# Head 1's keys and queries projected plainly, input sums spread over more steps, splits dealt by chunk, one copy moved to ScalarE

## The chip, the core and the metric

One core of a Trainium2 chip runs the whole program. Its engines are the matrix engine (PE, with its weight loads shown as PEld), VectorE (DVE), ScalarE (ACT), GpSimd (POOL) and SyncE (SP), which issues the transfers between memory and the on-chip buffers. PE writes only to PSUM banks; DVE and ACT read them out. Each engine runs its own instructions in order and waits on semaphores for the others. The metric is device time in microseconds, the median of the timed runs; less is better.

## The reference

An encoder of two layers on 1024 tokens of width 1024, in float32. Layer 0 mixes tokens by neighbourhood attention, layer 1 by differential attention; each layer then has a gated convolutional channel mixer and a gated embedding. The change lies in layer 1's attention:

```python
def diff_attention(h, w_qkv, lam, subln_g, w_o, t5_table, lambda_init):
    q, k, v = jnp.split(h @ w_qkv, 3, axis=-1)      # 8 heads; q, k: two maps of 64, v: 128
    ...
        s = jnp.einsum('bhmqd,bhmkd->bhmqk', qb, k).astype(jnp.float32) + bias[None, :, None]
        a = jax.nn.softmax(s, axis=-1)
        w = a[:, :, 0] - lam_full * a[:, :, 1]
        return jnp.einsum('bhqk,bhkd->bhqd', w.astype(v.dtype), v)
    ...
    o = rms_norm(o, subln_g) * (1.0 - lambda_init)
    return o @ w_o
```

## The kernel before

**Precision.** A float32 product is computed as three matmuls of a reduced-precision type (`mm3`, L258 to L263): each operand is split into a high part (ACT, `high`, L224) and a low remainder (DVE, `low`, L227), and high x high, high x low and low x high are accumulated in one PSUM bank. Splits thus cost ACT and DVE one instruction each.

**Two programs interleaved on PE.** PE's order is written out by hand; the other engines' order is found by the compiler, by priority (the order in the program) and by its own estimate of when an operand is ready. `da` runs the attention in 64 *chunks* n (8 heads of 8 blocks of 128 queries): the scores of chunk n+1 (`da_scores`, L882), its softmax (DVE L704, ACT exponential L708, the difference of the two maps on DVE L895), the transposes of chunk n's weights in two groups of four (`da_turn`, L907; the first group copied out of PSUM by ACT, L910, the second by DVE, L912), the product with the values (`da_values`, L921, with ACT's squares L924, a DVE scalar L925, a POOL root L273 and a DVE scaling L927), and a transpose of the result (`da_out`, L935). Into it PE is given *steps* of the projections: `tick(part)` adds `part * self.rate` to a credit and takes one step of the generator `da_stream` for each whole unit of it. The rate is 6.5 steps a chunk for the first 16 chunks and 5.14 behind. A step is one `mm3` (L261, L262, L263), 512 tokens wide. `need` takes steps at once until a head's keys and queries (`self.qk`) or values (`self.v`) exist.

**The stream before.** `plain` projects one weight block by one half of the tokens in 8 steps. Head 0's keys and queries are plain (32 steps), then the values of heads 0 and 1 (32 steps). The rest is done in *pairs* (`PAIRS`): a pair of weight blocks is multiplied in 7 half-size products of 4 steps instead of 8 (a Strassen-like scheme), 28 steps for what takes 32. A pair's products need sums of weight quarters (`Pair.sums`, four POOL operations, L118 to L121), splits of seven stationary operands (`Pair.operand`), and sums of the outputs (`put`, L158 to L175). They also need twelve sums of input quarters, T1 to T4, made once, in `sums(n)`: POOL operations (L560 to L570) into `room`, splits into a ring of four slots, a store to memory (`stash`, L554), from where each pair loads them again (L616). `sums(0)` to `sums(8)` were called at fixed steps of the plain part: steps 18, 26, 30, 36, 42, 46, 52, 57 and 61, counted from the stream's start. Each call first emits the splits and stores of the sums of the call before.

**Jobs.** `self.jobs` is a list of small pieces of work (a split, say). `job(act, dve)` takes the first one and orders its ACT part behind the instruction `act` and its DVE part behind `dve`. Before, it is filled near the layer's end only (rows of the output weights, the embedding's operands) and called in two places a chunk: behind the difference of the maps (in `da_scores`) and behind the second copy (in `da_turn`). `hurry` takes a job at once.

**Turns.** Values come out of the projection transposed; a *turn* (L292, and a copy on ACT, L590) brings them to rows. Turns wait a given number of steps and then for the end of a chunk or for `need`.

Of the kernel before, what the change touches and what calls it, by code (L numbers as in the profile page):

```python
# [92 lines left out]
PAIRS = [("kq", 1), ("kq", 2), ("v", 2), ("kq", 3), ("kq", 4), ("v", 4), ("kq", 5), ("kq", 6), ("v", 6), ("kq", 7)]  # L93
# [5 lines left out]
class Pair:  # L99


    def __init__(self, trunk, W, room, kind, j):
        self.trunk, self.room, self.kind, self.j = trunk, room, kind, j
        self.src = (W[KT + j], W[j]) if kind == "kq" else (W[2 * KT + j], W[2 * KT + j + 1])
        self.A, self.o, self.ps = {}, {}, {}
        self.products = [PRODUCTS[n] for n in range(7)]

# [15 lines left out]
    def operand(self, q):  # L123
        k = self.products[q][0]
        self.o[k] = self.trunk.operand(self.A[k])
# [14 lines left out]
    def out(self, row, half, src, turns, turn, wait):  # L140

        k, j = self.trunk, self.j
        if self.kind == "v":
            turns.append([wait, turn(self.h[row], half, src, 2 * (j + row) + half)])
            return
        s = slice(half * 512, half * 512 + 512)
        if row:
            k.split(src, self.h[:, 0, s], self.h[:, 1, s], -0.125)
        else:
            k.split(src, self.h[:, 2, s], self.h[:, 3, s])  # L150

    def put(self, a, turns, turn):
# [12 lines left out]
        elif a == "S3":  # L165
            tt(out=w, in0=ps[1], in1=p1, op=ALU.add)
        elif a == "S1":
            act(c5, ps[2], AF.Copy)
            nc.gpsimd.tensor_tensor(out=w, in0=w, in1=c5, op=ALU.add)
            self.out(1, 1, w, turns, turn, 4)  # L170
        elif a == "A22":
            tt(out=p1, in0=ps[1], in1=p1, op=ALU.add)
            self.out(1, 0, p1, turns, turn, 3)
        else:
            tt(out=u, in0=ps[2], in1=u, op=ALU.add)  # L175
            self.out(0, 1, u, turns, turn, 3)
            if self.kind == "kq":
                self.trunk.qk[self.j] = self.h


class Trunk:
# [329 lines left out]
    def da_stream(self, hT, x, first, mid):  # L511
# [4 lines left out]
        turns = []  # L516

# [8 lines left out]
        def plain(w, tb, wait=None):  # L526
            s = slice(tb * 512, tb * 512 + 512)
            ps = self.bank(self.pj)
            for kt, _ in enumerate(self.proj(w, hT, ps, tb)):
                if wait:  # L530
                    wait(kt)
                step()
# [40 lines left out]
        def at(*steps):  # L573
            steps = dict(steps)
            return lambda kt: sums(steps[kt]) if kt in steps else None

        s, ps = yield from plain(wk, 0)
        self.split(ps, A[:, 2, s], A[:, 3, s])
        s, ps = yield from plain(wq, 0, mid)
        self.split(ps, A[:, 0, s], A[:, 1, s], -0.125)  # L580
        s, ps = yield from plain(wk, 1, at((2, 0)))
        self.split(ps, A[:, 2, s], A[:, 3, s])
        wv = self.wblock(W[2 * KT])
        s, ps = yield from plain(wq, 1, at((2, 1), (6, 2)))
        self.split(ps, A[:, 0, s], A[:, 1, s], -0.125)
        self.qk[0] = A

        def turn(v, g, src, way):
            def of():
                self.transposed(src, lambda _, t: nc.scalar.activation(v[:, 4 * g : 4 * g + 4], t, AF.Copy), groups=(0,))  # L590
                self.v[way] = v
            return of

        steps = [at((4, 3)), at((2, 4), (6, 5)), at((4, 6)), at((1, 7), (5, 8))]
        for j in range(2):
            v = self.page(x, "v", (P, KT, P), bufs=3)
            vT = self.page(self.raw, "raw")
            for tb in (0, 1) if j == 0 else (1, 0):
                s, ps = yield from plain(wv, tb, steps.pop(0))
                nc.scalar.activation(vT[:, s], ps, AF.Copy)  # L600
                turns.append([5, turn(v, tb, vT[:, s], 2 * j + tb)])
                if j == tb == 1:
                    for k in range(4):
                        self.split(room[:, k], B12[0][:, k], B12[1][:, k])
                    pairs = [Pair(self, W, room, *a) for a in PAIRS]
                    pairs[0].load(0), pairs[0].load(1)
                    pairs[0].sums()
            if j == 0:
                wv = self.wblock(W[2 * KT + 1])

        moving = {"B11": B11, "B21": B21, "T1": B12, "B22": B22}
# [8 lines left out]
        for k in range(4):  # L620
            load(k)
        for n in range(3):
            pairs[0].operand(n)
        for i, p in enumerate(pairs):
            last = i == len(pairs) - 1
            after = None if last else pairs[i + 1]
            p.begin(x)
            for q, (a, b, bank) in enumerate(p.products):
                if after and q == 5:
                    after.sums()  # L630
                if q + 3 < 7:
                    p.operand(q + 3)
                elif after:
                    after.operand(q - 4)
                if after and q in (1, 2):
                    after.load(q - 1)
                if last and q == 0:
                    emb = self.embeddings(1, x)
                if last and q in (0, 6):
                    next(emb)  # L640
                ps, first = p.bank(bank, q)
                for k in range(4):
                    mov = (ring[:, k, 0], ring[:, k, 1]) if b in stash else tuple(o[:, k] for o in moving[b])
                    o = p.o[a]
                    self.mm3(ps, (o[:, 0, k], o[:, 1, k]), mov, first and k == 0, k == 3, not first)
                    if b in stash:
                        load(k)
                    step()
                    yield
                p.put(a, turns, turn)  # L650

        yield
# [7 lines left out]
    def begin(self, stream):  # L660
        self.stream, self.qk, self.v, self.credit, self.rate, self.open = stream, {}, {}, 0.0, 6, False
        self.jobs = []
# [204 lines left out]
    def da_scores(self, x, n):  # L867
# [27 lines left out]
        done = nc.vector.scalar_tensor_tensor(out=w, in0=e[1], scalar=c, in1=w, op0=ALU.mult, op1=ALU.add).ins  # L895
        self.job(self.exp, done)

    def da_turn(self, x, n, g):
# [10 lines left out]
        if g == 0:  # L909
            self.turned_w = nc.scalar.activation(wT[:, 0:4], t, AF.Copy).ins  # L910
        else:
            self.job(self.turned_w, nc.vector.tensor_copy(wT[:, 4:8], t).ins)  # L912

    def da_values(self, x, n):
# [31 lines left out]
    def da(self, hT, oT, first, mid):  # L946
# [4 lines left out]
        with self.tc.tile_pool(name="xa1", bufs=2, reuse_waits="tile") as x:  # L951
# [5 lines left out]
            for n in range(N + 1):  # L957
                self.rate = 6.5 if n < 2 * NT else 5.14
# [95 lines left out]
    def hurry(self):  # L1054

        todo = self.jobs.pop(0)
        if todo:
            todo()

# [989 lines left out]
```

## Time and profile before

| what | us |
|---|---|
| timed runs: median (lowest, highest) | 2711.51 (2711.2, 2711.7) |
| the profiled execution, its time | 2708.44 |
| the profiled execution, its span | 2706.7 |
| layer 1's attention, first chunk's scores to last chunk's | 1308.8 to 1877.4 |

The span runs from the first to the last instruction of the program on the core; the execution's own time adds 1.7 us around it. All times below are microseconds from the span's start. A matmul's listed duration is its latency; matmuls overlap, so the distance from one start to the next is what it costs PE. A wait is listed with what released it.

### The profile page before, as it was taken

How to read it: one execution, taken by the hardware profiler on the slowest of the kernel's cores; microseconds unless marked ns; L12 is line 12 of the kernel's file. 1: busy time of each engine (PE TensorE's matmuls, PEld its weight loads, DVE VectorE, ACT ScalarE, POOL GpSimd, SP SyncE). 2: the span in 40 equal slices, each digit the busy share in tenths (PEclk: the TensorE clock that was granted, in tenths of full speed). 3: DMA queues.
4: the chain of work that ended last, by engine and by line, in shares of the span. 5: the costliest groups of instructions: out<-in, count | busy, mean ns of one | idle time of the engine just before them, and what ended most of it. 6: DMA issues, size and time to landing. Idle time of an engine off the chain costs nothing.

```text
span 2706.7 us, 37008 instructions
## 1 busy us (share of the span) xinstructions
PE 2660.8 (98%) x13372; PEld 2196.0 (81%) x13372; DVE 2021.1 (75%) x3442; ACT 1353.2 (50%) x2548; POOL 561.2 (21%) x531
## 2 busy tenths in 40 slices
PE   8999999999999999999899999999999999999999
PEld 6888887878888888888678787777878888888887
DVE  6777776699777767676788888886699777768674
ACT  5555556454444444454455556565454444444452
POOL 2221220003334300001732222100103333300000
PEclk9999999999999999999899999999999999999999
DMA  6223226423332373333365555552423333374342
GB/s 184 85 66 105 76 94 195 132 71 128 106 113 98 116 272 122 117 131 115 124 240 200 197 175 194 178 171 91 160 70 131 103 108 103 103 261 138 117 137 100
DMA packets 151515, 367.21 MB, mean 136 GB/s; under 512 B 14202, under 2 KB 41082, under 8 KB 151331
## 3 DMA queue, kind: packets, MB, share of 16 engines
q1 hardware_dynamic: 151330, 364.85, 41.0%
q8 instruction: 105, 1.72, 0.3%
q14 instruction: 80, 0.65, 0.1%
HBM read 284.08 MB, written 92.90 MB: 139 GB/s over the span
## 4 chain that ended last, share of the span: by engine, by line
PE 38%; DVE 6%; ACT 2%; issue 2%; DMA 1%; POOL 1%; SPq 0%; ACTq 0%; DVEq 0%; POOLq 0%
PE b L261 9%; PE b L262 8%; PE b L263 8%; PE g L1078 3%; PE m L1078 3%; PE b L921 2%; PE s L882 2%; DVE E L704 1%; PE b L907 1%; DVE E L895 1%; ACT E L708 1%; PE b L1078 1%; PE b L292 1%; DVE ws L227 1%; DVE r L227 0%
## 5 line engine op out<-in xcount | busy, mean ns | idle before, releaser
L261 PE MATMUL b<-r,ws 128*128 128x512 f32 (+1 forms) x1304 | 532.3, 408 | 1.7 <-DVE r L396 1.6
L262 PE MATMUL b<-r,ws 128*128 128x512 f32 (+1 forms) x1304 | 505.2, 387 | 0.6 <-DVE r L227 0.5
L263 PE MATMUL b<-r,ws 128*128 128x512 f32 (+1 forms) x1304 | 505.6, 388 | 0.0
L263 PEld LDWEIGHTS b<-r,ws 128*128 128x128 f32 x1304 | 246.1, 189 | 51.3
L261 PEld LDWEIGHTS b<-r,ws 128*128 128x128 f32 x1304 | 247.4, 190 | 47.5 <-issue 3.5
L708 ACT ACTIVATE E<-E,mn 128x1024 f32<-128x1024 f32 (+2 forms) x256 | 221.7, 866 | 121.2 <-DVE mn L704 120.0
L262 PEld LDWEIGHTS b<-r,ws 128*128 128x128 f32 x1304 | 247.9, 190 | 35.5 <-DVE r L227 1.9
L261 PE MATMUL b<-r,wa 128*128 128x512 f32 x688 | 268.2, 390 | 2.0 <-DVE B L1470 2.0
L263 PE MATMUL b<-r,wa 128*128 128x512 f32 x688 | 268.1, 390 | 0.0
L262 PE MATMUL b<-r,wa 128*128 128x512 f32 x688 | 267.9, 389 | 0.0
L261 PE MATMUL b<-r,r 128*128 128x512 f32 x648 | 254.5, 393 | 0.9 <-ACT ws L1835 0.6
L262 PE MATMUL b<-r,r 128*128 128x512 f32 x648 | 252.7, 390 | 0.0
L263 PE MATMUL b<-r,r 128*128 128x512 f32 x648 | 252.5, 390 | 0.0
L273 POOL TENSOR_TENSOR ss<-ss,mhalf 128x1 f32<-128x1 f32 x128 | 74.3, 581 | 790.8 <-DVE ss L269 383.1
L224 ACT ACTIVATE r<-raw 128x512 fp32r<-128x512 f32 (+1 forms) x168 | 108.6, 655 | 192.0 <-PE b L262 168.9
L227 DVE TENSOR_TENSOR ws<-raw,ws 128x512 fp32r<-128x512 f32 (+3 forms) x178 | 168.2, 951 | 46.4 <-ACT ws L224 44.2
L227 DVE TENSOR_TENSOR r<-raw,r 128x512 fp32r<-128x512 f32 (+1 forms) x168 | 124.4, 747 | 71.0 <-ACT r L224 67.7
L224 ACT ACTIVATE ws<-raw 128x512 fp32r<-128x512 f32 (+3 forms) x178 | 122.1, 692 | 109.0 <-PE b L263 53.3
L1078 PE MATMUL m<-r,ws 128*128 128x512 f32 x672 | 157.0, 392 | 0.0
L1078 PE MATMUL g<-r,ws 128*128 128x512 f32 x672 | 155.8, 391 | 0.0
L261 PEld LDWEIGHTS b<-r,wa 128*128 128x128 f32 x688 | 129.2, 188 | 29.9 <-DVE B L1470 3.2
L704 DVE CUSTOM_DVE_ANT_0 E<-s,T 128x1024 f32<-128x1024 f32 x128 | 151.1, 1217 | 1.7 <-PE s L882 1.7
(226 smaller groups left out, 5384.0 us busy)
## 6 DMA issues: line engine op xcount, KB each, us to landing
r<-stashT SPq DMA_DIRECT2D x120, 512.0 KB, 4.3
raw<-in_w_in SPq DMA_DIRECT2D x86, 512.0 KB, 3.5
raw<-in_qkv SPq DMA_DIRECT2D x48, 512.0 KB, 5.1
spillS<-r SPq DMA_DIRECT2D x88, 256.0 KB, 3.0
r<-in_ffn_w_out SPq DMA_DIRECT2D x40, 512.0 KB, 5.9
raw<-spillS SPq DMA_DIRECT2D x40, 512.0 KB, 3.6
spillA<-B SPq DMA_DIRECT2D x66, 256.0 KB, 2.9
raw<-spillA SPq DMA_DIRECT2D x30, 512.0 KB, 3.9
```

The lines of the kernel that those rows point to most:

```text
L224: return self.nc.scalar.activation(hi, src, AF.Copy).ins
L227: return self.nc.vector.tensor_tensor(out=lo, in0=src, in1=hi.bitcast(F32), op=ALU.subtract).ins
L261: mm(out, sta[0], mov[0], start=first, stop=False, skip_group_check=onto)
L262: mm(out, sta[0], mov[1], start=False, stop=False, skip_group_check=onto)
L263: mm(out, sta[1], mov[0], start=False, stop=last, skip_group_check=onto)
L273: self.nc.gpsimd.tensor_tensor(out=ss, in0=ss, in1=self.mhalf, op=ALU.pow)
L292: self.nc.tensor.transpose(t[:, k * P : k * P + P], h[:, c : c + P], self.ident)
L704: nc.vector.tensor_tensor_reduce(out=e, in0=s, in1=bias, scale=1.0, scalar=3e38, op0=ALU.add, op1=ALU.min, accum_out=mn)
L708: self.exp = nc.scalar.activation(e, e, AF.Exp, bias=mn, scale=-1.0, accum_out=sm).ins
L882: nc.tensor.matmul(s[m][:, w], A[o, a, q], A[o, b, w], start=z == 0, stop=z == 2)
L921: nc.tensor.matmul(o, wT[:, k], V[:, k], start=k == 0, stop=k == KT - 1)
L1078: mm(out[half], a, b[:, w], start=first and k + z == 0, stop=last and k == n - 1 and z == 2)
```

## The change

- The pair `("kq", 1)` goes; head 1's keys and queries are projected by `plain`, between the values of head 0 and those of head 1 (whose halves are done in the order 1, 0). The plain part is now 96 steps long instead of 64, and nine pairs follow instead of ten.
- `sums(0)` to `sums(8)` are called at steps 18, 26, 35, 44, 53, 61, 69, 76 and 84. The splits and stores of the sums of the call before become jobs; what is left of them is emitted at the next call (`all_jobs`).
- The first pair's weights are loaded at steps 66 and 78, its first operand and the splits of one input quarter become jobs at step 88, its sums of weights are made at step 91. Every later operand is a job as well, asked for three products ahead as before; an operand that is not there when its product begins is made at once.
- While the stream is in its plain and pair part (`self.third`), `da_values` deals a job too, behind the squares, so there are three places a chunk; and the second copy of turned weights is done by ACT instead of DVE.
- The second load of a pair's weights is issued two products later, and the sum `w` is added by whichever of its two parts comes last.
- The rates are 6.3 and 5.3 instead of 6.5 and 5.14.

```diff
-PAIRS = [("kq", 1), ("kq", 2), ("v", 2), ("kq", 3), ("kq", 4), ("v", 4), ("kq", 5), ("kq", 6), ("v", 6), ("kq", 7)]
+PAIRS = [("kq", 2), ("v", 2), ("kq", 3), ("kq", 4), ("v", 4), ("kq", 5), ("kq", 6), ("v", 6), ("kq", 7)]
...
     def operand(self, q):
-        k = self.products[q][0]
-        self.o[k] = self.trunk.operand(self.A[k])
+        k, trunk = PRODUCTS[q][0], self.trunk
+
+        def do():
+            self.o[k] = trunk.operand(self.A[k])
+            return trunk.did
+
+        trunk.jobs.append(do)
...
+        def put(m, key, t):
+            did = self.split(t, ring[:, m % 4, 0], ring[:, m % 4, 1])
+            nc.sync.dma_start(stash[key][m // 3], raw[:, m % 4])
+            return did
+
         def sums(n):

             k = n // 2
+            self.all_jobs()
             if made:
-                for m, key, t in made.pop():
-                    self.split(t, ring[:, m % 4, 0], ring[:, m % 4, 1])
-                    nc.sync.dma_start(stash[key][m // 3], raw[:, m % 4])
+                self.jobs += [lambda a=a: put(*a) for a in made.pop()]
...
+        plan = {u: lambda n=n: sums(n) for n, u in enumerate((10, 18, 27, 36, 45, 53, 61, 68, 76))}
+        plan |= {58: lambda: pairs[0].load(0), 70: lambda: pairs[0].load(1), 80: first_operands, 83: first_sums}
...
+        yield from keys(wk, A, 0)
+        yield from queries(wq, A, 0, mid)
+        yield from keys(wk, A, 1)
+        ws.append(self.wblock(W[2 * KT]))
+        yield from queries(wq, A, 1)
+        self.qk[0] = A
+        yield from values(ws.pop(), 0, (0, 1), W[KT + 1])
+        A = self.page(self.r2, "r2", (P, 4, SEQ), F32R)
+        wk = ws.pop()
+        yield from keys(wk, A, 0)
+        wq = self.wblock(W[1])
+        yield from keys(wk, A, 1)
+        yield from queries(wq, A, 0)
+        wv = self.wblock(W[2 * KT + 1])
+        yield from queries(wq, A, 1)
+        self.qk[1] = A
+        yield from values(wv, 1, (1, 0))
+        pairs[0].operand(2)
...
+            if after and q == 3:
+                self.all_jobs()
+                after.load(1)
+            if after and q == 5:
+                self.all_jobs()
+                after.sums()
+            if n + 3 < len(order):
+                order[n + 3][0].operand(order[n + 3][1])
...
+            while a not in p.o:
+                self.hurry()
...
         if g == 0:
             self.turned_w = nc.scalar.activation(wT[:, 0:4], t, AF.Copy).ins
+        elif self.third:
+            self.job(nc.scalar.activation(wT[:, 4:8], t, AF.Copy).ins, self.meant)
         else:
             self.job(self.turned_w, nc.vector.tensor_copy(wT[:, 4:8], t).ins)
...
-        nc.scalar.activation(os, o, AF.Square, scale=r0, accum_out=r)
-        nc.vector.tensor_scalar(out=r, in0=r, scalar1=1.0 / P, scalar2=EPS, op0=ALU.mult, op1=ALU.add)
+        squared = nc.scalar.activation(os, o, AF.Square, scale=r0, accum_out=r).ins
+        meant = nc.vector.tensor_scalar(out=r, in0=r, scalar1=1.0 / P, scalar2=EPS, op0=ALU.mult, op1=ALU.add).ins
         self.root(r)
+        if self.third:
+            self.job(squared, meant)
+        self.meant = meant
...
-                self.rate = 6.5 if n < 2 * NT else 5.14
+                self.rate = 6.3 if n < 2 * NT else 5.3
```

(The step numbers in `plan` are counted from the stream's ninth step.)

More of the change, by code (lines that the diff above doesn't have):

```diff
@@ L104, in __init__ @@
         self.src = (W[KT + j], W[j]) if kind == "kq" else (W[2 * KT + j], W[2 * KT + j + 1])
-        self.A, self.o, self.ps = {}, {}, {}
-        self.products = [PRODUCTS[n] for n in range(7)]
+        self.A, self.o, self.ps, self.made, self.w = {}, {}, {}, [], 0
     def load(self, n):
@@ L571, in sums @@
                 made.append([(3 * k + 1, "T3", t3), (3 * k + 2, "T4", t4)])
[L573 to L611, printed above, removed]
+        pairs = [Pair(self, W, room, *a) for a in PAIRS]
+        units = []
         loads = [k for _ in pairs for k in ("T2", "T3", "T4")]
@@ L619, in da_stream, with first_operands, first_sums @@
         todo = [0] * 4
[L620 to L624, printed above, removed]
+        def first_operands():
+            self.all_jobs()
+            self.jobs += [lambda k=k: self.split(room[:, k], B12[0][:, k], B12[1][:, k]) for k in range(4)]
+            pairs[0].operand(0)
+            for k in range(4):
+                load(k)
+        def first_sums():
+            self.all_jobs()
+            pairs[0].sums()
+            pairs[0].operand(1)
@@ new lines, in values @@
+        def values(w, j, halves, then=None):
+            v = self.page(x, "v", (P, KT, P), bufs=3)
+            vT = self.page(self.raw, "raw")
+            for tb in halves:
+                s, ps = yield from plain(w, tb)
+                nc.scalar.activation(vT[:, s], ps, AF.Copy)
+                turns.append([5, turn(v, tb, vT[:, s], 2 * j + tb)])
+                if then:
+                    ws.append(self.wblock(then))
+                    then = None
+        ws = []
+        yield from keys(wk, A, 0)
@@ L625, in da_stream @@
+        yield from queries(wq, A, 1)
+        self.qk[1] = A
+        yield from values(wv, 1, (1, 0))
+        pairs[0].operand(2)
+        moving = {"B11": B11, "B21": B21, "T1": B12, "B22": B22}
+        order = [(p, q) for p in pairs for q in range(7)]
+        for n, (p, q) in enumerate(order):
+            i = pairs.index(p)
             last = i == len(pairs) - 1
             after = None if last else pairs[i + 1]
[L627 to L650, printed above, removed]
@@ new lines, in da_stream @@
+            if last and q in (0, 6):
+                next(emb)
+            while a not in p.o:
+                self.hurry()
+            ps, first = p.bank(bank, q)
+            for k in range(4):
+                mov = (ring[:, k, 0], ring[:, k, 1]) if b in stash else tuple(o[:, k] for o in moving[b])
+                o = p.o[a]
+                self.mm3(ps, (o[:, 0, k], o[:, 1, k]), mov, first and k == 0, k == 3, not first)
+                if b in stash:
+                    load(k)
+                step()
+                yield
@@ L652, in da_stream @@
+            p.put(a, turns, turn)
+        self.third = False
         yield
```

51 lines of the change are left out of this document (43 added, 8 removed).

## The prediction

> **What bounds the kernel now.** I read the page first: span, engine shares, the 40 slices.
>
> ```profile
> span 2706.7 us, 37008 instructions
> PE 2660.8 (98%) x13372; PEld 2196.0 (81%) x13372; DVE 2021.1 (75%) x3442; ACT 1353.2 (50%) x2548; POOL 561.2 (21%) x531
> PE   8999999999999999999899999999999999999999
> PEclk9999999999999999999899999999999999999999
> ```
>
> The matrix engine (PE) sets the end almost everywhere, so a step that removes PE work or a PE gap is worth its full length, and one that relieves another engine only what a gap hides. In the row of slices one place past the first is low both in busy share and in granted clock: slice 20, where layer 1's attention begins. The change works there and in the 570 us behind it.
>
> The PE's price of a *step* (three 128x512 matmuls, one tick of the stream) comes from the timeline of a quiet stretch: from one L261 to the next.
>
> ```profile
> 1289.79 0.39 PE L261 MATMUL b<-r,ws 128*128 128x512 f32 x1
> 1290.47 0.39 PE L261 MATMUL b<-r,ws 128*128 128x512 f32 x1
> ```
>
> That is 0.68 us a step; the 0.39 is latency, overlapped. Next, the view of busy time by stretch, for line L261 alone (its count is the number of steps), L292 (transposes of values) and L912 (one for each chunk). I cut the stretches at the scores (L882) that open a chunk.
>
> ```profile
> 1318.80:1354.50 35.70, 8.51 (x16) 4.16 (x16) 0.81 0.43 164
> 1354.50:1365.20 10.70, 2.69 (x6) 1.19 (x6) 1.00 0.86 302
> 1402.10:1413.10 11.00, 2.99 (x7) 1.32 (x7) 1.00 0.41 137
> 1413.10:1476.80 63.70, 19.60 (x45) 8.49 (x45) 1.00 0.62 213
> 1495.20:1833.40 338.20, 90.46 (x204) 38.73 (x204) 1.00 0.55 182
> 1833.40:1844.30 10.90, 2.24 (x5) 0.94 (x5) 1.00 0.46 176
> ```
> ```profile
> 1318.80:1354.50 35.70, 1.26 (x8) 0.92 (x8) 0.81 0.43 164
> 1354.50:1365.20 10.70, 0.65 (x4) 0.42 (x4) 1.00 0.86 302
> 1413.10:1476.80 63.70, 1.19 (x8) 1.00 (x8) 1.00 0.62 213
> 1495.20:1833.40 338.20, 4.88 (x32) 3.75 (x32) 1.00 0.55 182
> ```
> ```profile
> 1413.10:1476.80 63.70, 4.79 (x7) 1.00 0.62 213
> 1495.20:1833.40 338.20, 27.39 (x40) 1.00 0.55 182
> ```
>
> Four transposes take 0.44 us, by the chain of waits in a stretch where PE itself is the chain:
>
> ```profile
> 1407.37 0.44 PE b L907 x4
> ```
>
> The fourth stretch is clean: 7 chunks, 45 steps, 8 transposes in 63.7 us. So a chunk's own PE work costs (63.7 - 45 x 0.68 - 0.9) / 7 = 4.6 us. With 4.6 a chunk and 0.68 a step, the others should have taken, and lost:
>
> - chunks 1 and 2 (35.7 us): 9.2 + 10.9 + 0.9 = 21.0, **lost 14.7**; mean clock 0.81
> - chunk 3 (10.7): 4.6 + 4.1 + 0.4 = 9.1, lost 1.6
> - chunk 8 (11.0): 4.6 + 4.8 = 9.4, lost 1.6
> - chunks 18 to 57 (338.2): 184 + 138.7 + 3.5 = 326.2, **lost 12.0**, 0.3 a chunk
> - chunk 58 (10.9): 4.6 + 3.4 = 8.0, lost 2.9
>
> What stood in the way in chunks 1 and 2 is in the view of waits for that stretch:
>
> ```profile
> ACT r L224 <- DMA stashT<-r: 7.0, 1, 7.0
> ACT r L224 <- POOL r L568: 4.1, 1, 4.1
> PEld b L907 <- ACT wT L910: 4.0, 1, 4.0
> PEld b L921 <- ACT v L590: 2.9, 1, 2.9
> ```
>
> ACT runs in order. Splits of the input sums (L224) sit at its head and wait, once for GpSimd (POOL) to finish a sum, once for a ring slot still being stored. Behind them stands the copy of turned weights (L910), without which PE gets no bank for its transposes (L907), and a copy of values (L590). The gap then lowers the clock. The sums and splits themselves fit neither engine for that stretch:
>
> ```profile
> 1318.80:1354.50 35.70, 27.06 (x130) 21.21 (x129) 31.04 (x36) 17.40 (x33) 31.57 (x21) 0.81 0.43 164
> 1495.20:1833.40 338.20, 331.79 (x2126) 267.23 (x2126) 280.75 (x542) 206.44 (x426) 61.23 (x68) 1.00 0.55 182
> ```
>
> (columns: PE, PEld, DVE, ACT, POOL.) DVE is 87% and POOL 88% busy in the first, 83% and 18% in the long one.
>
> **The change part by part.** *Head 1 plain.* The durations, from the groups of 1476.8 to 1800 us (count, busy us, mean ns), and the loads of the page:
>
> ```profile
> L227 DVE TENSOR_TENSOR ws<-raw,ws 128x512 fp32r<-128x512 f32 x19 | 13.0, 682 | 0.0
> L224 ACT ACTIVATE ws<-raw 128x512 fp32r<-128x512 f32 x19 | 11.8, 621 | 0.1
> L160 DVE TENSOR_TENSOR r<-b,r 128x512 f32<-128x512 f32 x7 | 4.8, 685 | 0.0
> ```
> ```profile
> r<-stashT SPq DMA_DIRECT2D x120, 512.0 KB, 4.3
> ```
>
> A pair is 7 products of 4 steps, 28; plain is 4 halves of 8, 32. Four steps more, on the bounding engine with nothing to hide them: **+2.7 us**, whatever else happens. DVE loses 7 operand splits and 4 sums of about 0.68 and gains two splits twice as wide (about 1.4 each): 5 us less, counted below. The four output splits stay. SP loads the same two weight blocks and 12 stash loads fewer (108 instead of 120); DMA is never the wait outside the burst, so nothing.
>
> *Sums spread.* Nine calls that stood at steps 18 to 61 now stand at 18 to 84. POOL's work does not change, 36 operations:
>
> ```profile
> L568 POOL TENSOR_TENSOR r<-r,r x4: 1267/1280/2265, 1321.9 to 1349.2; 128x512 f32<-128x512 f32 x4
> L895 DVE SCALAR_TENSOR_TENSOR E<-E,c,E x64: 1259/1266/2345, 1315.2 to 1883.5; 128x1024 f32<-128x1024 f32 x64
> ```
>
> At 1.3 to 2.3 us, a call of four or five takes 5 to 11 us. The calls were 4 to 6 steps apart, which at 6.5 steps in a 9.0 us chunk is 5.5 to 8.3 us: less than POOL needs when slowed. Now they are 7 to 9 steps apart, 9.7 to 12.6 us at 6.3 steps in 8.9 us: POOL ends a sum before its split is asked for. The ring's slots, used again after four splits, get the same slack for the store.
>
> *Splits dealt.* Each split and store is a job put behind a chunk's exponential, its turned copy or its squares, three places a chunk, instead of where the stream asks. ACT no longer meets a sum that isn't ready ahead of L910. The order adds no data wait; behind a dealt split that waits anyway stand the copies of the next half chunk. Cover: twelve steps of lead, two chunks, for an operand. If it is gone the PE waits, at most the 0.62 + 0.68 of one split each time.
>
> Together these two take the cause of the 16.3 us lost in chunks 1 to 3. Not all returns: chunk 1 still calls for head 0's values as soon as they exist, and DVE stays near 85% for eleven chunks. Least recovery is nothing (the stall moves along), most 16.3. I leave 1.3 for the values and 0.3 (the long stretch's loss) for each of eleven chunks, 4.6: **-11.7**, nearer the full end because the two waits that make the gap lose their reason. Chunk 8 waits for head 1's last keys and queries. They were ready at step 92, and the scores call after 48 + 6.5 x 7 = 93 (33 steps stand ahead of the first scores, 12 behind them, 3 are called for head 0's values: 48); now at step 80: **-1.6** (bounds 0 and -1.6).
>
> *The copy on ACT.* L912 leaves DVE:
>
> ```profile
> L912 DVE COPY wT<-b x64: 677/684/694, 1328.8 to 1887.5; 128x512 f32<-128x512 f32 x64
> L910 ACT ACTIVATE wT<-b x64: 578/598/601, 1326.0 to 1885.8; 128x512 f32<-128x512 f32 x64
> ```
>
> 40 x 0.68 = 27 us less for DVE in the long stretch (83% to 75%), 24 more for ACT (61% to 68%). It is on the path of the values' products (L921), which need it from their second half:
>
> ```profile
> 1411.38 1.78 PE b L921 x16
> ```
>
> 0.9 us after they start. Two chunks of the timeline show where ACT would have it, behind the second exponential:
>
> ```profile
> 1499.45 1.15 ACT L708 ACTIVATE E<-E,mn 128x1024 f32<-128x1024 f32 x1
> 1501.62 1.95 PE L921 MATMUL b<-v,wT 128*128 128x128 f32 x16
> 1659.70 1.13 ACT L708 ACTIVATE E<-E,mn 128x1024 f32<-128x1024 f32 x1
> 1660.39 2.05 PE L921 MATMUL b<-v,wT 128*128 128x128 f32 x16
> ```
>
> In the first the exponential ends at 1500.6, the copy would at 1501.2, wanted at 1502.5: 1.3 us to spare. In the second 1660.8, 1661.4, wanted at 1661.3: 0.1 late; there DVE's splits had held up the scores, and these the change puts behind. So the 12.0 us of the long stretch may go, or double. I take half, **-6**, the chunk with room being the common one; bounds -12 and +12 (0.3 more in each of 40).
>
> *Values of later heads.* The pairs now start at step 96, not 64, with one fewer. Head 2's values are turned by step 96 + 56 + 3 = 155; chunk 17 calls at 48 + 16 x 6.3 + 5.3 = 154. Before: 64 + 84 + 4 = 152 against 157. Heads 4 and 6 likewise: 239 against 239, 323 against 324. So three heads now call for values just being turned: four transposes, 0.44, and the copy:
>
> ```profile
> L590 ACT ACTIVATE v<-b x16: 578/586/598, 1330.5 to 1765.5; 128x512 f32<-128x512 f32 x16
> ```
>
> About 1.0 each: **+3** (bounds 0 and 3 x 2.9, the wait above). Rates 6.3 and 5.3 give 355 steps against 351, as the work does: the tail and its 2.9 us stay.
>
> **Sum:** 2.7 - 11.7 - 1.6 - 6 + 3 = -13.6. The profiled execution took 2708.4 us, so 2694.8; the median of the three timed runs, 2711.5, lies 3.1 above, so **2698**.
>
> One rule of the Trainium skill speaks against spreading, "SBUF — State Buffer", section "Who interferes with whom": a DVE instruction with two SBUF inputs contends with a GpSimd instruction that reads SBUF. The trace agrees: L895, with two SBUF inputs, takes 1.27 alone and up to 2.35, L568 1.28 and up to 2.27. By it the spread lets four more chunks' L895 collide, 0.9 us each, and the sum would be 2702 (it lies within the first rival's price).
>
> **The rivals.**
> - *The burst is only thinned* (18%). DVE was 87% busy in the burst; over eleven chunks it still has own work and splits, and POOL at work slows L895 by up to 1.08 us. If each of the eleven chunks loses 0.8 instead of 0.3 (+5.5) and the long stretch keeps its 12 (+6), the time is 2709 or so. For it: L895's maximum. Against: the wait that made the gap was ACT's, not DVE's load. That dealing does nothing, the compiler's order being much the same, gives this too.
> - *Everything goes* (16%): the long stretch loses 10 of its 12 and the values' waits are hidden: 2691.
> - *The ACT copy becomes the bound* (8%). In each of some 53 chunks the second half of L921 waits behind two exponentials and perhaps a dealt split. It decides when the second exponential ends later than 0.3 us after L921's start (0.9 less the copy's 0.6); with a split ahead, 0.62 sooner. At 0.6 a chunk, +32 in place of the -6: slower, 2736. For it: the chunk at 1660. Against: that at 1501, and DVE freed sooner.
>
> **How the numbers follow.** Forecast 58%, rivals 18, 16 and 8%. The measurement tells 0.2% apart, 5.4 us: faster means under 2706.1, slower over 2716.9. Faster: nearly all of the forecast, the third case, a third of the second: 79%. Same: the rest of these, 13%. Slower: the last, 8%. The range takes in the third case with 5 us for what the long stretch's lower bound may add, and the second with 2: 2686 to 2711; the slow case lies outside.
>
> **What would show it.** Steps in the layer's attention up by 4 (L261 x4 more). Chunks 1 and 2 near 21 to 23 us, clock 1.00, no ACT wait for the stash or for POOL over 2 us. L910 with twice the count, no L912 until the last chunks. Values waiting for L590 at chunks 17, 33 and 49. The long stretch's loss under 8 us. Wrong if PE waits for the ACT copy in most chunks, or if the first eleven chunks together still lose over 10.

## The result and the profile after

The changed kernel is slower by a little, clear of the noise: 2718.35 us median of 10 runs beside 2711.02 of the kernel before, ratio 1.0027 (95% 1.0017 to 1.0037). 2698 was forecast. The profiled executions took 2721.1 us (2.75 above its median) and 2708.44 (2.6 below), so between the two traces 5 of the 12.6 us of span are chance.

The page of the changed kernel, its span, two rows of busy time and two of the slices:

```profile
span 2719.3 us, 36972 instructions
PE 2665.1 (98%) x13384; PEld 2197.9 (81%) x13384; DVE 1970.9 (72%) x3379; ACT 1373.0 (50%) x2595; POOL 561.5 (21%) x526
PE   8999999999999999999999999999999999999999
PEclk9999999999999999999999999999999999999999
```

DVE does 50 us less work, the dip of slice 20 is gone, and still the end came later. Next the changed kernel by stretch: all engines (PE, PEld, DVE, ACT, POOL, granted clock), then its steps (L268) and transposes of values (L299).

```profile
1319.60:1346.00 26.40, 21.20 (x129) 16.41 (x128) 18.78 (x26) 13.32 (x25) 22.27 (x15) 1.00 0.45 160
1382.50:1397.20 14.70, 11.20 (x60) 8.76 (x58) 10.59 (x16) 6.50 (x14) 5.51 (x4) 0.88 0.43 154
1493.30:1803.20 309.90, 302.53 (x1937) 244.76 (x1936) 227.64 (x453) 196.98 (x414) 70.95 (x67) 1.00 0.57 190
1803.20:1870.40 67.20, 60.42 (x364) 48.38 (x363) 50.76 (x94) 44.84 (x89) 3.83 (x7) 0.95 0.36 123
```
```profile
1382.50:1397.20 14.70, 3.71 (x7) 1.76 (x7) 0.88 0.43 154
1493.30:1803.20 309.90, 83.88 (x190) 36.01 (x190) 1.00 0.57 190
```
```profile
1493.30:1803.20 309.90, 4.93 (x32) 3.67 (x32) 1.00 0.57 190
```

What a stretch lost is again its length less PE's own work, with 4.587 us a chunk, 0.681 a step and 0.109 a transpose (the prediction's three prices, one digit more). Chunk 7 (second row): 14.7 - 4.6 - 7 x 0.681 = 5.3. Chunks 18 to 53 (third row): 309.9 - 165.1 - 129.4 - 3.5 = 11.9. In the same way, for most of the profiled executions (us lost; e1 to e17 are the experiments; each column is one execution, and e6's took 4.9 us more than e6's median):

| chunks | before | after | e1 | e4 | e6 | e7 | e8 | e9 | e14 | e15 | e16 | e17 |
|---|---|---|---|---|---|---|---|---|---|---|---|---|
| 1 to 3 | 16.4 | 6.3 | 5.6 | 10.5 | 19.3 | 7.4 | 6.8 | 10.2 | 5.6 | 6.3 | 15.4 | 6.1 |
| 4 to 11 | 2.0 | 9.1 | 5.5 | 4.3 | 5.2 | 8.6 | 6.1 | 2.1 | 6.9 | 6.9 | 3.0 | 3.2 |
| 12 to 17 | 0.3 | 1.4 | 0.2 | 0.7 | 0.7 | 2.0 | 2.0 | 0.2 | 0.1 | 0.2 | 0.2 | 0.1 |
| 18 to 53 | 10.3 | 11.9 | 5.7 | 13.0 | 16.2 | 19.1 | 11.3 | 5.7 | 6.6 | 7.4 | 6.3 | 5.8 |
| 54 to 62 | 6.0 | 11.5 | 8.0 | 11.2 | 9.9 | 7.4 | 11.2 | 11.1 | 11.1 | 9.7 | 6.0 | 9.5 |

A gain is there: 10.1 us in chunks 1 to 3, and chunk 8's 1.6. It is given back: 5.3 in chunk 7, 3.4 in the rest of chunks 4 to 11, 1.1 in chunks 12 to 17, 5.5 behind chunk 53, and 1.6 in chunks 18 to 53, where most of 6 were to be won. The rest of the 12.6 us: six more steps inside the chunks (359 beside 353, 4.1 us; two of them had stood in the tail), 0.8 ahead of the first chunk, and 2.7 behind the last chunk's start, where the experiments lie up to 2.4 apart.

Who waits is in PE's waits of the attention; three of the longest sums of the changed kernel (us in all, times, longest):

```profile
PE b L988 <- DVE os L980: 7.7, 4, 3.5
PE b L971 <- ACT wT L960: 4.0, 7, 1.0
PE b L299 <- ACT wT L960: 2.5, 2, 1.7
```

L988 is the transpose of a chunk's result (`da_out`), L980 its scaling on DVE, L960 the copy that went to ACT. Rows of the timeline of chunk 7 show where the first one's 3.5 us come from (DVE's, and PE's wait):

```profile
1383.46 2.99 DVE L234 TENSOR_TENSOR r<-r,r 128x512 fp32r<-128x512 f32 x3
1386.38 0.14 DVE L975 TENSOR_SCALAR ss<-ss 128x1 f32<-128x1 f32 x1
1386.44 1.71 DVE L234 TENSOR_TENSOR r<-r,r 128x512 fp32r<-128x512 f32 x1
1388.08 1.21 DVE L750 CUSTOM_DVE_ANT_0 E<-s,T 128x1024 f32<-128x1024 f32 x1
1390.36 0.40 DVE L980 TENSOR_SCALAR os<-b,sum,ss 128x128 f32<-128x128 f32 x1
1390.82 0.33 PE L988 MATMUL b<-ident,os 128*128 128x128 f32 x1 [3.50 <-DVE os L980]
```

Four halves of splits (L234) stand in DVE's queue, three ahead of the chunk's mean (L975) and one behind it; the scaling (L980) comes after them and two L750. They became jobs at step 88, three steps before `first_sums` empties the list (`all_jobs`) at step 91: they were flushed, not dealt.

### The profile page after: what moved, and what is told of

Its sections match the earlier page's. It is cut to its first block, busy times and chain, and to the rows that moved or that the text cites. A ratio compares the mean times of both kernels' runs of the same rounds, so it can differ in the third digit from the quotient of the medians.

```text
span 2719.3 us, 36972 instructions
## 1 busy us (share of the span) xinstructions
PE 2665.1 (98%) x13384; PEld 2197.9 (81%) x13384; DVE 1970.9 (72%) x3379; ACT 1373.0 (50%) x2595; POOL 561.5 (21%) x526
## 4 chain that ended last, share of the span: by engine, by line
PE 82%; DVE 7%; ACT 5%; issue 2%; POOL 2%; DMA 1%; SPq 0%; ACTq 0%; DVEq 0%; POOLq 0%
PE b L268 19%; PE b L269 19%; PE b L270 19%; PE g L1135 6%; PE m L1135 5%; PE b L971 3%; ACT E L754 2%; PE s L928 2%; PE b L299 2%; PE b L1135 2%; PE av L821 2%; PE b L955 1%; PE b L794 1%; DVE E L750 1%; DVE r L234 1%
## 5 line engine op out<-in xcount | busy, mean ns | idle before, releaser
L268 PE MATMUL b<-r,ws 128*128 128x512 f32 (+1 forms) x1308 | 533.2, 408 | 1.7 <-DVE r L403 1.7
L754 ACT ACTIVATE E<-E,mn 128x1024 f32<-128x1024 f32 (+2 forms) x256 | 221.5, 866 | 148.3 <-DVE mn L750 148.1
L268 PEld LDWEIGHTS b<-r,ws 128*128 128x128 f32 x1308 | 247.8, 189 | 47.6 <-issue 3.3
L269 PEld LDWEIGHTS b<-r,ws 128*128 128x128 f32 x1308 | 248.3, 190 | 35.6 <-DVE r L234 1.9
L268 PE MATMUL b<-r,wa 128*128 128x512 f32 x688 | 268.1, 390 | 1.9 <-DVE B L1527 1.9
L280 POOL TENSOR_TENSOR ss<-ss,mhalf 128x1 f32<-128x1 f32 x128 | 83.6, 654 | 857.7 <-DVE ss L276 382.1
L268 PE MATMUL b<-r,r 128*128 128x512 f32 x648 | 254.4, 393 | 1.3 <-DVE facc L1731 0.7
L231 ACT ACTIVATE r<-raw 128x512 fp32r<-128x512 f32 (+1 forms) x168 | 108.7, 655 | 195.4 <-PE b L269 169.9
L234 DVE TENSOR_TENSOR ws<-raw,ws 128x512 fp32r<-128x512 f32 (+3 forms) x177 | 170.8, 971 | 49.6 <-ACT ws L231 48.0
L231 ACT ACTIVATE ws<-raw 128x512 fp32r<-128x512 f32 (+3 forms) x177 | 122.3, 697 | 109.0 <-PE b L270 52.0
L234 DVE TENSOR_TENSOR r<-raw,r 128x512 fp32r<-128x512 f32 (+1 forms) x168 | 124.8, 749 | 70.3 <-ACT r L231 67.3
L268 PEld LDWEIGHTS b<-r,wa 128*128 128x128 f32 x688 | 129.1, 188 | 29.9 <-DVE B L1527 3.2
L750 DVE CUSTOM_DVE_ANT_0 E<-s,T 128x1024 f32<-128x1024 f32 x128 | 151.1, 1216 | 1.0 <-PE s L928 0.9
```

The lines of the kernel that those rows point to most:

```text
L231: return self.nc.scalar.activation(hi, src, AF.Copy).ins
L234: return self.nc.vector.tensor_tensor(out=lo, in0=src, in1=hi.bitcast(F32), op=ALU.subtract).ins
L268: mm(out, sta[0], mov[0], start=first, stop=False, skip_group_check=onto)
L269: mm(out, sta[0], mov[1], start=False, stop=False, skip_group_check=onto)
L280: self.nc.gpsimd.tensor_tensor(out=ss, in0=ss, in1=self.mhalf, op=ALU.pow)
L750: nc.vector.tensor_tensor_reduce(out=e, in0=s, in1=bias, scale=1.0, scalar=3e38, op0=ALU.add, op1=ALU.min, accum_out=mn)
```

## The experiments

Each kernel is compared with runs of the kernel before on the same chip. Differences between two experiments below are those of their medians; by their ratios most are 1 to 2 us smaller. First the parts of the change, one taken out at a time. *Theory A*: dealt and flushed splits stand in the chunk's chain on DVE. *Theory B*: the copy on ACT costs. *Theory C*: the fixed costs eat the gain.

**e1, the copy back on DVE**

```diff
-        elif self.third:
-            self.job(nc.scalar.activation(wT[:, 4:8], t, AF.Copy).ins, self.meant)
```

> One part of the change undone: the second copy of the turned weights is on VectorE again, everything else as after. Theory A (dealt and flushed splits stand on VectorE ahead of the mean's scaling and the output's scaling, and TensorE's turn of the output waits for it): the time stays at 2715 to 2721 us, and the waits of the output's turn for its scaling stay near 7.7 us; with the copy back on VectorE they may grow. Theory B (the copy on ScalarE stands between the two exponentials, delays the second and with it the values' second half, for which TensorE waits): the time falls to 2711 us or less, and the two groups of TensorE's waits for the copy (4.0 and 2.5 us after) go. Theory C (only fixed costs: four more steps, 2.7 us, and the later heads' values): no change, 2718 us.

Measured 2704.67 us, ratio 0.9982 (0.9973 to 0.9991). The copy, with the order that it gives to a dealt job (`job`'s first argument), turned a gain into a loss: 13.7 us (12 by the ratios). All stretches but chunk 7 profit.

**e2, no third place** (copy still on ACT), **e3, all splits at once**, **e4, both and the copy on DVE**

```diff
-        if self.third:
-            self.job(squared, meant)
```
```diff
-        trunk.jobs.append(do)
+        do()
...
-                self.jobs += [lambda a=a: put(*a) for a in made.pop()]
+                [put(*a) for a in made.pop()]
...
-            self.jobs += [lambda k=k: self.split(room[:, k], B12[0][:, k], B12[1][:, k]) for k in range(4)]
+            [self.split(room[:, k], B12[0][:, k], B12[1][:, k]) for k in range(4)]
```

> One part undone: no third place for a dealt job behind the mean's scaling, so a chunk takes at most the two jobs of before; the copy stays on ScalarE, the splits are still dealt. Theory A: if the third place is what puts a split ahead of the output's scaling, the time falls to about 2712 us and the waits of the output's turn fall from 7.7 to 2 to 4 us; the flush at step 91 (chunk 7, 5.3 us lost) stays or grows, since more is left over to flush. Theory B and theory C: no change, 2716 to 2720 us.

> One part undone: every split is issued at once where the kernel before issued it, none is dealt; the copy stays on ScalarE and the sums stay spread over 66 steps. Theory A: chunk 7 loses under 2 us instead of 5.3, chunks 54 to 60 lose 6 to 8 us instead of 11.5, and the time falls to 2708 to 2712 us. Theory B: no change, 2716 to 2720 us, and TensorE's waits for the copy on ScalarE stay at 6 to 7 us. Theory C: no change.

> Both schedulings undone: the copy is on VectorE, every split is issued at once, no third place. What stays is the plain projection of head 1, the sums spread over 66 steps, the values of later heads and the new rates. By the terms of the prediction that are left (2.7 of steps, 11.7 back from the first chunks, 1.6 from chunk 8, 3 for the later values) it takes 7.6 us less than before: about 2703 us. Theories A and B both forecast that (each 5 to 8 us of the distance to 2718 goes, the sum of both is 12 to 15). Theory C: the first chunks' gain is real but is given back by the steps and the later values, wherever the splits stand: 2714 to 2718 us.

Measured: e2 2721.55 us, 1.0044 (1.0031 to 1.0056); e3 2722.12, 1.0043 (1.0030 to 1.0056); e4 2714.66, 1.0018 (1.0009 to 1.0026). Theory A falls as stated: e2 and e3 lie above all that was expected of them. Their intervals overlap the changed kernel's, but with the copy on DVE it is clear that dealing and the third place help: from e4 to e1 they are worth 10.0 us. For e4, theories A and B forecast 2703; it lies in the range of theory C, but C doesn't explain the changed kernel, since e1 has the same fixed costs and is faster. Without the dealing, chunks 1 to 3 keep 10.5 of their loss. Plain projection and spread alone are a loss.

**e8, two places, copy on DVE** (e1 without the third place)

> On the kernel with the copy on VectorE (2704.67 us): no third place for a dealt job behind the mean, so at most two per chunk as before. With the copy on ScalarE the third place was worth 3.2 us (2721.55 without, 2718.35 with). If that holds here too: 2706 to 2710 us. Rival (the third place costs, since the split that it deals stands right ahead of the output's scaling for which TensorE's turn waits, 6.9 us in that kernel): 2699 to 2703 us.

Measured 2713.86 us, 1.0011 (1.0003 to 1.0020), above both expectations. The third place is worth 9.2 us (7.9 by the ratios), nearly all that the dealing gives. DVE's waits of chunks 18 to 53 say why: in the kernel before, in e8 and in e1,

```profile
DVE os L927 <- POOL ss L273: 28.8, 33, 1.9
DVE c L892 <- ACT E L708: 10.2, 20, 0.8
```
```profile
DVE os L976 <- POOL ss L280: 27.0, 31, 1.9
DVE c L938 <- ACT E L754: 15.6, 29, 1.2
```
```profile
DVE os L978 <- POOL ss L280: 7.2, 13, 0.7
DVE c L938 <- ACT E L754: 9.8, 23, 1.2
```

Without the third place DVE waits for POOL's root in nearly every chunk, about 0.9 us a time. The third place lies just there, between mean and scaling, and a split's low half (0.69 us) fills the hole: the wait falls from 27.0 to 7.2 us, and what these chunks lose from 11.3 to 5.7.

**e6, ACT's copy alone, on the kernel before** (same lines as in the change, nothing else)

> The kernel before with one thing of the change alone: the second copy of the turned weights on ScalarE in the chunks of the stream. Theory B (ScalarE's copy costs by itself, whatever is dealt): 8 to 14 us slower than before, 2718 to 2724 us. Rival (the copy costs only beside three dealt jobs, since their high parts queue on ScalarE with it): within 4 us of before. By the recorded prediction's reasoning it would be a few us faster.

Measured 2720.58 us, 1.0037 (1.0023 to 1.0051): it costs 10 us by itself. There are few jobs in this kernel's list before the layer's end, so the order of a dealt job has little part in it. Why should 0.58 us, on an engine that is busy 64% of the long stretch (196.98 of 309.9 in the changed kernel), cost that? DVE's waits in chunks 18 to 53, of the changed kernel (two rows) and of e6:

```profile
DVE c L938 <- ACT E L754: 40.8, 30, 2.3
DVE os L980 <- POOL ss L280: 10.8, 19, 1.9
```
```profile
DVE c L895 <- ACT E L711: 31.8, 27, 1.8
```

Against e1, the changed kernel's DVE does 24 us less (251.41 busy in e1) and waits 31.0 more for the exponential; in e6 the wait is 31.8 where the kernel before had 10.2. In both kernels ACT's order is first exponential, copy, second exponential, in all 36 of these chunks. The copy delays the second, and DVE's reciprocal, difference of maps and the next chunk hang on that. Three kernels ask which part of this costs.

**e7, both copies; e14, spare copies behind the exponential** (both on e1; the spare page is read by nobody)

```diff
...
+                nc.scalar.activation(spare, t[:, 0:2], AF.Copy)
+                self.job(nc.scalar.activation(spare, t[:, 2:4], AF.Copy).ins, done)
```
```diff
...
+                for k in (4, 6):
+                    spared = nc.scalar.activation(spare, wT[:, k : k + 2], AF.Copy).ins
+                    self.behind([spared], [self.exp])
+            self.job(self.turned_w, done)
```

> On the kernel with the copy on VectorE (2704.67 us): ScalarE besides copies the same turned weights, in two halves, into a spare page that nobody reads. Nothing waits for this copy but the bank it reads, so it costs ScalarE's time alone (a little over one copy's 0.58 us). If the copy costs because it stands in ScalarE's queue ahead of the second exponential and the high parts: 8 to 13 us slower than that kernel, 2713 to 2718 us. If it costs because TensorE's second half of the values waits for it directly: 0 to 4 us slower, 2705 to 2709 us.

> The kernel with the copy on VectorE (2704.67 us) and, besides, a spare copy of the same weights on ScalarE in two halves, as in the kernel that took 2722.02 us, but read from the turned page and placed behind the second exponential of the next chunk, and with the dealt high part not pinned behind it. If the place ahead of the second exponential (or the pin) is what costs: 2704 to 2709 us. If ScalarE's time is what costs, wherever it stands: 2714 to 2722 us.

Measured: e7 2722.02 us, 1.0042 (1.0029 to 1.0055); e14 2708.39, 0.9987 (0.9979 to 0.9996). So 17.4 us against 3.7, for about the same work on ACT (two copies of 0.38 us a chunk, and of 0.41). But e7 wasn't what its expectation took it for: the compiler put its copies behind the second exponential in all of chunks 18 to 53, as in e14. What is left between them is the page that is read, and that in e7 a job's ACT half was ordered behind the copy, as it is in the change. Nor does e7 lose its time where the change does: DVE's wait for the exponential is 16.3 us there (7.4 in e14), and PE's longest waits are for ACT's copy of a chunk's result (L1000), of which e14 has 0.3:

```profile
PE b L975 <- ACT ot L1000: 8.3, 11, 2.2
PE b L299 <- ACT ot L1000: 4.5, 6, 1.3
```

So e7 doesn't tell what the change paid for. e14 tells that ACT's time is cheap where it stands behind the second exponential. A kernel with the real copy at that place was not built.

**e15, the change without that order**

```diff
-            self.job(nc.scalar.activation(wT[:, 4:8], t, AF.Copy).ins, self.meant)
+            nc.scalar.activation(wT[:, 4:8], t, AF.Copy)
+            self.job(self.turned_w, self.meant)
```

> The changed kernel (2718.35 us) with one thing taken away: the dealt job's high part is placed behind the first copy of the turned weights, not behind the second copy on ScalarE, which stays there. If the pin is what costs: 2704 to 2710 us. If the copy's own place in ScalarE's queue costs: 2715 to 2721 us.

Measured 2710.74 us, 1.0004 (0.9995 to 1.0013). It fell just outside both expectations, because both hold in part: 7.6 of the 13.7 us are the order of the dealt half, 6.1 are left to the copy itself. (Of these 6.1 the profiles put 1.9 ahead of the first chunk, 1310.0 beside 1308.1, where the edit changes nothing, so they may be 4 or 5.) Another pair agrees: e3 and e4 deal no splits, so the order has nothing to hold there, and they differ by the copy's engine (and a third place that stays empty but near the end), 7.5 us. DVE's wait for the exponential stays at 35.6 us in e15, as the copy's place does. Rows of two timelines of the same chunks show the order's part: chunk 34 and the start of 35 in the changed kernel (chunk 35 loses 1.16 there), then in e15 (it loses nothing).

```profile
1633.70 1.15 ACT L754 ACTIVATE E<-E,mn 128x1024 f32<-128x1024 f32 x1
1634.85 0.57 ACT L960 ACTIVATE wT<-b 128x512 f32<-128x512 f32 x1
1635.32 1.14 ACT L754 ACTIVATE E<-E,mn 128x1024 f32<-128x1024 f32 x1
1636.45 0.62 ACT L231 ACTIVATE ws<-r 128x512 fp32r<-128x512 f32 x1
1637.25 0.68 DVE L234 TENSOR_TENSOR ws<-r,ws 128x512 fp32r<-128x512 f32 x1
1637.92 1.27 DVE L941 SCALAR_TENSOR_TENSOR E<-E,c,E 128x1024 f32<-128x1024 f32 x1
1638.01 2.33 POOL L116 TENSOR_TENSOR r<-raw 128x512 f32<-128x512 f32 x1 [5.93 <-DVE ws L234]
1640.41 1.28 POOL L117 TENSOR_TENSOR r<-r,raw 128x512 f32<-128x512 f32 x1
1640.54 1.70 DVE L234 TENSOR_TENSOR ws<-raw,ws 128x512 fp32r<-128x512 f32 x1 [0.37 <-ACT ws L231]
1642.69 0.41 DVE L980 TENSOR_SCALAR os<-b,sum,ss 128x128 f32<-128x128 f32 x1 [0.44 <-POOL ss L280]
```
```profile
1629.33 0.62 ACT L231 ACTIVATE ws<-r 128x512 fp32r<-128x512 f32 x1
1630.52 0.69 DVE L234 TENSOR_TENSOR ws<-r,ws 128x512 fp32r<-128x512 f32 x1
1631.29 1.29 POOL L116 TENSOR_TENSOR r<-raw 128x512 f32<-128x512 f32 x1 [3.41 <-DVE ws L234]
1632.66 1.28 POOL L117 TENSOR_TENSOR r<-r,raw 128x512 f32<-128x512 f32 x1
1636.34 0.69 DVE L234 TENSOR_TENSOR ws<-raw,ws 128x512 fp32r<-128x512 f32 x1 [0.37 <-ACT ws L231]
1636.94 0.40 DVE L981 TENSOR_SCALAR os<-b,sum,ss 128x128 f32<-128x128 f32 x1
```

Ordered behind the copy, the split's ACT half (L231) ran behind both exponentials (L754); its DVE half (L234) then missed the hole in which DVE waits for the second exponential (1630.52 in e15) and stood in front of the difference of the maps (L941). POOL's sums, released by it, came late as well and met the next split, which took 1.70 us instead of 0.69. It isn't this chunk alone: of the 46 weight splits dealt in chunks 18 to 53, the changed kernel has 16 with their ACT half behind both exponentials and ahead of the next squares, e15 and e1 have none.

**e9, sums at their old steps** (on e1), and **e16, the dealing alone on the kernel before**

```diff
-        plan = {u: lambda n=n: sums(n) for n, u in enumerate((10, 18, 27, 36, 45, 53, 61, 68, 76))}
+        plan = {u: lambda n=n: sums(n) for n, u in enumerate((10, 18, 22, 28, 34, 38, 44, 49, 53))}
```

> On the kernel with the copy on VectorE (2704.67 us): the nine input sums stand at the steps of before again (18 to 61 instead of 18 to 84), all else as there, head 1 still plain. If the spread is what takes the stall of chunks 1 to 3 away (16.4 us lost before, 5.6 there), these chunks lose 12 to 16 us again and the time is 2711 to 2716 us. If dealing alone had done it (with splits at once and the sums spread the chunks lost 10.5 to 13.2): 2705 to 2708 us.

> The kernel before with the dealing and the third place alone, copy on VectorE, head 1 in the first pair, sums at their old steps; the ring's first loads now stand behind the last dealt sums. If plain head 1 and the spread are needed for the first chunks: they lose 13 us or more in chunks 1 to 4 and the time is 2704 to 2709 us. If the dealing alone is enough: 8 us or less, 2698 to 2702 us.

Measured: e9 2706.52 us, 0.9984 (0.9976 to 0.9993); e16 2706.47, 0.9984 (0.9976 to 0.9993). In chunks 1 to 3 dealing alone leaves 15.4 lost, the plain head 1 with it 10.2, the spread as well 5.6: these two parts do there what they were credited with, the spread less than e9's expectation gave it (12 to 16). But in the total e9, e16 and e1 can't be told apart: the four steps, chunk 7 and the end take the gain, so the plain head 1 and the spread are worth nothing clear on the whole.

Three forerunners of e16 came before it:

> The kernel before with the dealing alone: stash splits, operands and the third place as after; head 1 stays in the first pair, the sums at their old steps, the copy on VectorE, the four splits of the first sum at once, the rates of before. If the dealing is the one part that gains, as the kernel with the sums at the old steps says (2706.5 us with four more steps, 2.7 us): 2700 to 2705 us. Rival (the plain head 1 is needed, since without it pair 0's operands and the second head's values fall due beside the dealt splits and wait): 2707 us or more.

> The dealing alone on the kernel before, and the embeddings' four half splits dealt too. By what each is held to be worth: 1 to 4 us below the dealing alone, 2697 to 2703 us; by the rival no difference between the two.

> The kernel before with the dealing and the third place alone, copy on VectorE, head 1 in the first pair, sums at their old steps. Each pair's second block is loaded two products later, behind the dealt operands, as after does. If the dealing with its third place carries the gain: 2702 to 2706 us and chunks 1 to 3 lose 8 to 11 us instead of 16.4. If plain head 1 is needed for it: 2707 to 2711 us, chunks 1 to 3 lose 13 us or more.

Measured: e10 2707.84 us, 0.9992 (0.9983 to 1.0000); e12 2711.18, 0.9999 (0.9990 to 1.0008); e13 2707.36, 0.9989 (0.9980 to 0.9997). In these three the ring's first loads stand ahead of the last two dealt sums (in e10 and e12 a pair's second block is also loaded ahead of a dealt operand), so the pairs multiply other numbers, with the same instructions and sizes. They agree with e16 on the long stretch (6.3 lost in each), and are used for nothing else.

**e5, a later flush** (on e1), **e11, the embeddings' splits dealt too** (on e5), **e17, the last sums earlier as well** (on e1)

```diff
-        plan |= {58: lambda: pairs[0].load(0), 70: lambda: pairs[0].load(1), 80: first_operands, 83: first_sums}
+        plan |= {58: lambda: pairs[0].load(0), 70: lambda: pairs[0].load(1), 79: first_operands, 86: first_sums}
```

> On the kernel with the copy back on VectorE (2704.67 us, 0.9982 of before): the four splits of the first sum are queued one step earlier and the sums that overwrite their source are made three steps later, so that the splits are dealt and at most two of five jobs are flushed. If the flush at step 91 is what costs chunk 7 its 5.2 us, chunk 7 loses under 1.5 us, a neighbouring chunk at most 1.5, and the time falls to 2699 to 2702 us. Rival: pair 0's sums are now late and its second product waits for them on GpSimd: the 5 us turn up in chunks 8 and 9, and the time stays at 2703 to 2706 us.

> On the kernel with the copy on VectorE and the later flush (2703.31 us): the four half splits of the embeddings' last operands, which chunk 54 issues at once (its VectorE runs 2.49 us of them ahead of the mean and TensorE's turn waits 2.2 us), are dealt too. If such a burst is what costs chunk 54 its 2.4 to 4.0 us: chunk 54 loses under 1 us and the time is 2699 to 2701 us. Rival (they are late for the next product instead, or turn up in chunks 55 to 57): no change, 2702 to 2705 us.

> The kernel with the copy on VectorE, the last sums a little earlier (the ninth at step 76, not 84), the first operands queued at step 83 and the sums that overwrite their source at step 92, so that the five jobs between them find five or six places. If chunk 7's 5.2 us were the flush: chunks 7 to 9 lose under 2 us together, chunks 1 to 3 stay at 5 to 7 us, and the time is 2698 to 2702 us. Rival (the burst's work is late wherever it stands): chunks 7 to 11 lose 3 us or more, 2702 to 2706 us.

Measured: e5 2703.31 us, 0.9972 (0.9962 to 0.9982); e11 2706.71, 0.9986 (0.9978 to 0.9995); e17 2704.63, 0.9980 (0.9971 to 0.9989). In e5 chunk 7 loses nothing: the flush was its cause. But chunk 9 loses 2.8, in e17 chunk 8 2.0, so about half of it is work that is late somewhere, and both times lie in the ranges of their rivals. Dealing the embeddings' splits brought nothing: chunks 54 to 62 lost 13.2 in e11 and 11.2 in e5. e5 has the lowest median of both kernels and all experiments, 7.2 us under the kernel before, but the intervals of e1, e9, e16, e17 and others overlap its own.

## Why the prediction was wrong, step by step

- **Four steps, +2.7**: right (4.1 inside the chunks, with two steps taken from the tail).
- **The first eleven chunks, -11.7, and chunk 8, -1.6**: the cause was right in chunks 1 to 3 and 8, the sum was not. Chunks 1 to 3 gave 10.1 us back and chunk 8 its 1.6. But the term covers chunks 1 to 11, and there 15.4 us were lost beside 18.4, a gain of 3.0 where 13.3 were forecast; "the first eleven chunks together still lose over 10", a sign of being wrong, is what came. Chunk 7's flush takes 5.3 of it, and the copy most of the 3.4 in chunks 4 and 9 to 11: with the copy on DVE (e1) chunks 4 to 11 lose 0.3 outside chunk 7. Chunks 1 to 3 need all three parts (e4, e9, e16); the clock is 1.00 in the row of 1319.6 us, though chunks 1 and 2 take 26.4 us and not the 21 to 23 announced. One wait stayed, though "no ACT wait for POOL over 2 us" was announced: ACT's first split of a sum in chunk 1 waits 5.4 us for POOL (L584), and L299 1.9 us for the first copy behind it.
- **The long stretch, -6: the step that failed is "The copy on ACT".** It placed the copy behind the second exponential and asked only whether the values would find it late. In the run the copy stands ahead of the second exponential, in all 36 chunks, and the prediction did not ask who stands behind it in ACT's queue: the second exponential and, by `job`, the ACT half of a split. That cost 13.7 us where 6 were to be won (e1), 7.6 of them by the order of the dealt half (e15). PE's waits for the copy are 6.5 us; DVE, which was relieved of 24 us in chunks 18 to 53, waited 31 more for the exponential. That the rest of the 13.7 goes this way is read from the waits; in no run did the copy alone change its place. Chunks 18 to 57, the stretch of the prediction, lost 20.6 us instead of 12.0. In chunks 18 to 53 the loss did fall to about half, 5.7, where the copy stays on DVE (e1), but by splits in holes, not by less work on DVE.
- **Splits dealt, "at most the 0.62 + 0.68 of one split"**: wrong where `all_jobs` empties the list; the five jobs that were queued three steps before cost 5.3 us in chunk 7.
- **Values of later heads, +3**: oversized. Chunks 17, 33 and 49 lost 0.69, 0.67 and 0.62, before 0.24, 0.31 and 0.59: +0.8.
- **"The tail and its 2.9 us stay"**: wrong; chunks 54 to 62 lost 5.5 more, and 1.4 to 7.2 more in the kernels with plain head 1 and the copy on DVE. The 2.9 of chunk 58 fell to 0.6, but chunk 54 lost 4.4 (before 1.5) and chunk 57 3.4 (0.2), with clocks of 0.86 and 0.89. With head 1 in the first pair (e16) the loss is 6.0, as before. In chunk 54 four splits of the embeddings' operands stand together on DVE; they end 0.8 us later in the chunk than before (the mean that follows them starts 3.45 us after the scores in e1, 2.62 in the kernel before). Dealing them didn't help (e11), and why the end costs more than before stays open.
- **The third rival** named the right edit at 8%, by another path: PE waits for the copy nine times, not in most chunks, so its price of 32 us was too high. The first rival had two signs right, the loss of the first eleven chunks and the 12 us that the long stretch keeps, but not for its reason: e1 has the same sums and GpSimd work and loses neither to that extent (11.1 in the first eleven chunks, 5.2 of it the flush; 5.7 in chunks 18 to 53).
- **A slip in the working**: 7 to 9 steps at 6.3 steps in 8.9 us are 9.9 to 12.7 us, not 9.7 to 12.6. Nothing hangs on it.

Without the copy the time comes nearer: e1 took 6.7 us more than the forecast, and chunk 7 and the end, which the prediction didn't see, cost 7.2. That these agree is luck in part: the 6 us credited to the copy came, nearly, by the dealing.

## What to carry to other kernels

When work is moved to a less busy engine in an in-order pipeline, ask what stands behind it in that queue and who waits for that; the mean share of busy time doesn't tell. An explicit order (`behind`) moved along with an instruction can cost as much as the instruction itself (here 7.6 us beside 6.1). Deal small work into the places where the engine waits anyway (here DVE's waits for POOL's root and for the second exponential), and leave no list to be flushed a few steps after it was filled.

## What the hardware showed unexpectedly

The same wait cost 2.4 us once and 4.0 another time. Chunk 54 of e1 and of e5, whose PE wait is the same 2.2 us (L986 for L978), then 2 us slices around it (first column behind the length: PE; third number from the end: granted clock):

```profile
1790.20:1800.60 10.40, 8.20 (x53) 6.61 (x52) 9.68 (x19) 6.34 (x14) 0.55 (x1) 1.00 0.42 128
1794.00:1796.00 2.00, 0.29 (x3) 0.05 (x1) 2.00 (x3) 1.00 (x1) 0.52 (x1) 1.00 0.88 302
1798.00:1800.00 2.00, 2.00 (x16) 1.84 (x16) 1.94 (x3) 0.82 (x2) 0.00 (x0) 1.00 0.11 34
```
```profile
1788.20:1800.20 12.00, 9.80 (x53) 8.00 (x52) 9.68 (x19) 6.35 (x14) 0.55 (x1) 0.86 0.36 111
1792.00:1794.00 2.00, 0.30 (x3) 0.07 (x1) 2.00 (x3) 0.99 (x1) 0.53 (x1) 1.00 0.94 338
1796.00:1798.00 2.00, 2.00 (x7) 1.62 (x7) 1.95 (x3) 0.83 (x2) 0.00 (x0) 0.50 0.11 34
1798.00:1800.00 2.00, 2.00 (x14) 2.00 (x13) 0.00 (x0) 0.00 (x0) 0.00 (x0) 0.66 0.00 0
```

In e5 PE is idle for 2.2 us (1792.3 to 1794.5), and the clock halves after it is back at work: (1 - 0.50) x 2 + (1 - 0.66) x 2 = 1.7 us lost, the difference of the two chunks (12.0 - 10.4 = 1.6). The Trainium skill, "TensorE: Matmul & The Clock Gate", section "What's actually happening", says that the gate judges PE's activity in windows that run freely and don't start with the kernel. Such windows could be why an equal gap was punished in one run and not in the other; no run here shows the windows, nor how much of one has to be idle. In the changed kernel the clock was 0.88, 0.86 and 0.89 in chunks 7, 54 and 57, which is 1.3 to 1.8 us each. If chance decides on these, differences of about 3 us between single profiles of these kernels say little.
